# A hybrid attention trunk on one core: gate sums, logits and 1/rms from split fp32r parts, Silu and 1/rms by Ln and Exp

## The chip, the cores and the metric

The kernel runs on one core of one Trainium2 chip. The metric is the device time in microseconds (us) of one execution, and lower is better. TensorE (PE in the profile) multiplies matrices, VectorE (DVE) and ScalarE (ACT) work on tiles element by element, GpSimd (POOL) fills tiles and issues some loads, SyncE (SP) issues the loads of the large weights. TensorE's products land in PSUM, eight banks of 128 partitions by 512 fp32 columns; the other tiles live in SBUF.

## The reference

The input x has 512 tokens of 1024 features. Two layers run; every layer is FFN, mixer, FFN, each on a normed input and each added to x. The mixer is a gated linear attention (GLA) in layer 0 and a stick-breaking attention (SB) in layer 1. The last step is one more norm.

```python
def rmsnorm(x, g):
    y = x * lax.rsqrt(jnp.mean(x * x, axis=-1, keepdims=True) + EPS)
    return y * g

def swiglu(h, w_gate, w_up, w_down):
    return (jax.nn.silu(h @ w_gate) * (h @ w_up)) @ w_down

def gla_mixer(h, w_in, w_gk2, b_gk, o_norm, w_out):
    q, k, v, g, gk_lr = jnp.split(h @ w_in, [512, 1024, 2048, 3072], axis=-1)   # gk_lr: 16 columns
    log_a = jax.nn.log_sigmoid(gk_lr @ w_gk2 + b_gk) / 16.0
    ...                                     # four heads: o from q, k, v and the decay exp(cumsum(log_a))
    o = rmsnorm(o, o_norm)                  # over the 256 features of each head
    return (o * jax.nn.silu(g)) @ w_out
```

## The kernel before

**Layout.** x is held transposed: eight tiles `xs[k]` of 128 features by 512 tokens. A weight column block is the stationary operand of a product, the tokens are its moving operand, so a product has 512 columns. A norm needs a sum over features, which lie on partitions; that sum is made on TensorE with a tile of ones.

**Split operands.** A matrix product of fp32 values is made from three products of fp32r parts (`mm3`, line 66): an operand a is cast to fp32r (`high`), and `low` = a - high is the rest; high x high, low x high and high x low are added up in PSUM. ScalarE casts a weight block (line 124, `wh<-raw`) and VectorE subtracts (line 126, `wl<-raw,wh`). Some small products stay in plain fp32, among them the sums over features, the gate logits and the products inside the heads.

**The queue of weight blocks.** `Feed` holds a list of entries in order: each loads its block, splits it and multiplies. `feed.step` makes one part of the entry at the front, `feed.entries` makes whole entries, `two_halves` makes the first two of a stage in two halves each, so that the part that needs the later features comes last. Loads and splits run three to six entries ahead. Stages that have a chain of their own (the heads of the GLA, the SB) take steps of the feed in between, to keep TensorE supplied. The order in which the instructions of an engine are laid down comes from a scheduler at build time, by priority and by its own view of durations; on the chip each engine then works through its queue in that order.

**PSUM.** `psum(name, tag)` takes a page under the tags "a" (2 banks), "z" (3), "t" (2) and "o" (1); without a tag it goes round all eight in turn (line 47).

**The norm of a stage.** While the last product of a stage updates x, `prep` (line 368) multiplies x by the gain of the next norm, splits it, and `sumsq` (line 359) adds up the squares in `ss`. The next stage multiplies the un-normed input first and scales its first results by R, the 1/rms of each token spread over all partitions. `stats_a` (line 381) makes R's values: four products of `ss` with a ones column (ps_st, 512 tokens as 4 columns of 128 partitions), then `rstd` on tiles of 4 columns (Sqrt on ScalarE, reciprocal and one Newton step on VectorE). `stats_b` (line 421) spreads them: four 128x128 diagonal tiles `dg` times ones (ps_R), and a copy to `R`. This is done in each of six stages; the first FFN takes the sums from elsewhere.

**An FFN stage** (`FFN.run`, line 696) calls `two_halves(stats_a)`, `stats_b`, then scales the two products that waited, and in `normed_input` (line 644) makes the normed, split tiles that entries from the seventh on use (`nh`, `nl`).

**The GLA stage** (`GLA.run`, line 980). `gate_weights` loads the small gate weights by POOL. `gate_low` multiplies the 16 gate columns (ps_gk); they lie in rows 0 to 15 (high part of the weight) and 32 to 47 (low part). `gate_logits` multiplies by R into `ga` and makes the logits with the plain fp32 tile `w2` (ps_z, four products of 512 columns); row 64 is 1 for the bias. `evac_q`, `evac_k`, `evac_g` scale the products of a feature block (ps_f, tag "a") by R. q of heads 0 and 1 are the two that wait for R (`defer`), so they hold both banks "a". For each head, `levels` computes the scores in seven steps, `output` the head's result: squares, their sum by ones (ps_on, plain fp32, 512 columns), 1/rms by Ln, Exp and a Newton step, and the normed result `on`. `silu` (line 965) applies Silu to all eight gate tiles `gn` in head 3's turn, and `close` (line 971) multiplies `on` by `gn` and splits the product for `back`, the out projection (ps_b).

ScalarE holds one set of function tables at a time; a function from another set needs an `ACT_TABLE_LOAD`. `act` (line 459) keeps Exp and Ln behind the load of the set that has both.

Of the kernel before, what the change touches and what calls it, by code (L numbers as in the profile page):

```python
# [10 lines left out]
F32 = mybir.dt.float32  # L11
# [21 lines left out]
def decoder(ctx: ExitStack, tc: tile.TileContext, a: dict, out: bass.AP):  # L33
# [23 lines left out]
    gT = cp.tile([P, 51], F32, name="gT")  # L57
    nc.vector.memset(gT[:, 50:51], 1.0)
    ones = gT[:, 50:51].to_broadcast([P, P])

    xs = [xp.tile([P, T], F32, name=f"x{k}") for k in range(KD)]

# [71 lines left out]
    class Feed:  # L134
# [17 lines left out]
            e = self.q[i]  # L152
            return e.body(e.W)

        def step(self, n=1):
            while n > 0:
                if self.cur is None:
                    self.cur = self.start()
# [262 lines left out]
    def stats_b(tag=None):  # L421
# [12 lines left out]
        st["R"] = sp.tile([P, T], F32, tag="sq", name="R")  # L434
        nc.vector.tensor_copy(st["R"], ps)

    def two_halves(between=None):

        feed.finish()
        g = [feed.start(), feed.start()]  # L440
        for i in range(3):
            for x in g:
                next(x, None)
            if i == 0 and between is not None:
                between()
# [19 lines left out]
    class FFN:  # L465
# [9 lines left out]

        def __init__(self, wg, wu, wd, gi, nxt, first=False, last=False):
            self.gi, self.normed = gi, False
            self.defer, self.gates = [], []
            self.lead = []
            self.hs = [[] for _ in self.GROUPS]  # L480
            base, downs = len(feed.q), []
            self.sums_by = 10**6
            for group, (c0, c1) in enumerate(self.GROUPS):
                slots, put = 2 * (c1 - c0), 0
                if group == 1:

                    for put in range(self.AHEAD):
                        down(*downs[put], late=put == 0)
                    put = self.AHEAD
                for i in range(slots):  # L490
# [24 lines left out]
                    while c >= self.SEVEN and put < len(downs) * (i + 1) // slots:  # L515
                        down(*downs[put])
                        put += 1
                for x in downs[put:]:
                    down(*x)
                n = 2 * (c1 - c0)  # L520
                end = group + 1 == len(self.GROUPS)
                downs = [(wd, c0 * 256, n, self.hs[group], part, nxt if end else None) for part in range(n)]
            self.count = len(feed.q) - base
            if last:
                back_tok(wd, c0 * 256, n, self.hs[group], nxt)
            else:
                for x in downs:
                    down(*x)
            self.total = len(feed.q) - base
# [166 lines left out]
        def run(self, between=None):  # L696
            with tc.tile_pool(name="hp", bufs=8, reuse_waits="tile") as self.hp, tc.tile_pool(
# [1 line left out]
            ) as self.tp:  # L699
                st["few"] = self.hp  # L700
                new_norm()
                two_halves(stats_a)
                stats_b()
                flush(self.defer)
                def spread(todo, n):
                    for i in range(n):
# [21 lines left out]
    class GLA:  # L728
        def __init__(self, w_in, w_gk2, b_gk, og, w_out, nxt):
# [7 lines left out]
                feat(chunks[h // 2], h % 2, lambda ps: self.evac_q(h, ps), "a", self.defer if h < 2 else None)  # L737

            def kk(h):
                feat(chunks[2 + h // 2], h % 2, lambda ps: self.evac_k(h, ps), "a")  # L740

            qk(0), qk(1), kk(0), kk(1), qk(2), qk(3), kk(2), kk(3)
            for c in range(4):
# [25 lines left out]
        def evac_g(self, j, ps):  # L769
            self.gn[j] = self.gp.tile([P, T], F32, tag="g", name="gn")  # L770
            nc.vector.tensor_tensor(out=self.gn[j], in0=ps, in1=st["R"], op=ALU.mult)

        def gate_weights(self):

            gr = self.ep.tile([P, KD, 16], F32, tag="gr", bufs=1, name="gr")
            with nc.allow_non_contiguous_dma("gate columns"):
                nc.gpsimd.dma_start(gr, cols(self.w_in, 3072, 16))
            self.gs = gs = self.ep.tile([P, KD, P], F32R, tag="gs", bufs=1, name="gs")
            nc.gpsimd.memset(gs.bitcast(F32), 0.0)
            nc.scalar.copy(gs[:, :, 0:16], gr)  # L780
            nc.vector.tensor_tensor(
                out=gs[:, :, 32:48], in0=gr, in1=gs[:, :, 0:16].bitcast(F32), op=ALU.subtract
            )
            self.w2 = w2 = self.gp.tile([P, T], F32, tag="g", name="w2")
            nc.gpsimd.memset(w2, 0.0)
            nc.gpsimd.dma_start(w2[0:16], self.w_gk2)
            nc.gpsimd.dma_start(w2[32:48], self.w_gk2)
            nc.gpsimd.dma_start(w2[64:65], self.b_gk)
            self.tri = self.ep.tile([P, P], F32, tag="tri", bufs=1, name="tri")
            nc.gpsimd.dma_start(self.tri, a["c_tri"])  # L790
            lf = self.ep.tile([P, len(LEVELS) * P // 2], F32, tag="e", name="lf")
            nc.gpsimd.dma_start(lf, a["c_lvl"])
            self.lvl = self.ep.tile([P, len(LEVELS) * P // 2], U8, tag="lvl", bufs=1, name="lvl")
            nc.vector.tensor_copy(self.lvl, lf)
            self.ga = self.gp.tile([P, T], F32, tag="g", name="ga")
            nc.gpsimd.memset(self.ga[64:65], 1.0)

        def gate_low(self):
            self.psg = psum("ps_gk", "z")
# [2 lines left out]
                mm(self.psg, self.gs[:, k], st["l"][k], False, k == KD - 1)  # L802

        def gate_logits(self):
            nc.vector.tensor_tensor(
                out=self.ga[0:64], in0=self.psg[0:64], in1=st["R"][0:64], op=ALU.mult
            )
            self.la = []
            for i in range(NT):
                ps = psum("ps_z", "z")  # L810
                mm(ps, self.ga[0:65, i * P : (i + 1) * P], self.w2[0:65], True, True)
                t = self.gp.tile([P, T], F32, tag="g", name="la")
                nc.scalar.activation(t, ps, AF.Abs)
                act(t, t, AF.Exp, scale=-1.0)
# [70 lines left out]
        def output(self, h):  # L885
# [40 lines left out]
            for vb in range(2):  # L926
# [18 lines left out]
            nc.vector.tensor_scalar(  # L945
                out=vv, in0=ps, scalar1=1.0 / 256, scalar2=EPS, op0=ALU.mult, op1=ALU.add
# [15 lines left out]
                self.on[j] = t  # L962
            yield

        def silu(self):
            for j in range(KD):
                with tc.issue_after(st["last"]):
                    s = nc.scalar.activation(self.gn[j], self.gn[j], AF.Silu).ins
            exp_ln_tables(s)

        def close(self, h):
            for j in (2 * h, 2 * h + 1):
                nc.vector.tensor_tensor(out=self.on[j], in0=self.on[j], in1=self.gn[j], op=ALU.mult)
# [2 lines left out]
                nc.scalar.copy(hh, self.on[j])  # L976
                nc.vector.tensor_tensor(out=hl, in0=self.on[j], in1=hh.bitcast(F32), op=ALU.subtract)
                self.hs.append((hh, hl))

        def run(self):  # L980
            with ExitStack() as es:
# [17 lines left out]
                self.decay(0)  # L999
                self.decay(1)  # L1000
                prev = None
                for h in range(4):
                    if h == 1:
                        self.decay(2)
                        self.decay(3)
                    for n, _ in enumerate(self.levels(h)):
                        feed.step(1)
                        if prev is not None and n >= 1:
                            next(prev, None)
                            if n == 4:  # L1010
                                feed.step(1)
                    if prev is not None:
                        for _ in prev:
                            feed.step(1)
                    prev = self.output(h)
                    if h == 3:
                        while feed.pos < self.end:
                            feed.step(1)
                        feed.finish()
                        next(prev)  # L1020
                        self.silu()
                        for g in range(3):
                            self.close(g)
                for n, _ in enumerate(prev):
                    if n < 6:
                        feed.step(1)
                self.close(3)
                feed.entries(self.end + 2 - feed.pos)


# [338 lines left out]
```

## Time and profile before

| | us |
|---|---|
| median of 3 runs (1864.43 to 1865.8) | 1865.71 |
| the profiled execution | 1867.25 |
| its span, from the first to the last instruction | 1865.3 |
| PE busy | 1845.7 |
| DVE busy | 1409.8 |
| ACT busy | 1009.2 |

| stage | us from the span's start |
|---|---|
| first FFN | 0 to 351 |
| GLA | 351 to 595 |
| FFN, FFN | 595 to 933, 933 to 1271 |
| SB | 1271 to 1517 |
| last FFN and output | 1517 to 1865 |

A row of the timeline has the start, the duration, the engine, the line, the operation, output and inputs by name, the shapes, and how many were merged; a bracket says how long the engine had been idle before and what ended it. A product in plain fp32 leaves two records, one in fp32r leaves one; PEld is the load of the stationary operand, which overlaps the products. A group row ends with busy time and mean ns of one, then the idle time before the group and what ended it. Products are pipelined: each lasts longer in its record than its distance to the next, so the price of one in a stream is that distance.

### The profile page before, as it was taken

To read this page: it belongs to the slowest core of one execution; us is meant where nothing else is said; L and a number is where in the kernel's file an instruction comes from. 1 tells how busy PE (TensorE), PEld (TensorE's weight loads), DVE (VectorE), ACT (ScalarE), POOL (GpSimd) and SP (SyncE) were. 2 spreads that over 40 slices of the span, in tenths; PEclk is the share of its full clock that TensorE was granted. 3 is DMA by queue.
4 is the path that set the end of the run, shared out by engine and by line. 5 is a ranking of instruction groups with operands and counts; after the bars stand their busy time and mean duration, and the time that the engine had idled before them with its cause. 6 is when DMAs were issued, how large, how long until landed. Compare 5 with 4: busy or idle time off the path is not lost.

```text
span 1865.3 us, 29157 instructions
## 1 busy us (share of the span) xinstructions
PE 1845.7 (99%) x11945; PEld 1650.8 (88%) x11945; DVE 1409.8 (76%) x2171; ACT 1009.2 (54%) x1708; POOL 7.3 (0%) x17
## 2 busy tenths in 40 slices
PE   8999999999999999999999999999999999999998
PEld 6999999789888899999889999998888788999997
DVE  7987776675767987777788777676878669877775
ACT  6545445444555554544564445445888745554454
POOL 0000000000000000000000000000000000000000
PEclk9999999999999999999999999999999999999999
DMA  5343333211223233332243333233221222333321
GB/s 159 113 131 107 102 113 111 80 52 62 66 70 112 78 105 116 110 115 80 84 131 102 103 108 108 80 93 100 68 69 57 69 90 91 125 102 102 118 87 68
DMA packets 177513, 179.04 MB, mean 96 GB/s; under 512 B 4034, under 2 KB 167924, under 8 KB 177380
## 3 DMA queue, kind: packets, MB, share of 16 engines
q1 hardware_dynamic: 176768, 176.18, 29.7%
q8 instruction: 93, 1.52, 0.3%
q0 software_dynamic: 512, 0.99, 0.2%
q14 instruction: 40, 0.33, 0.1%
q10 hardware_dynamic: 100, 0.03, 0.0%
HBM read 175.11 MB, written 2.10 MB: 95 GB/s over the span
## 4 chain that ended last, share of the span: by engine, by line
PE 95%; DVE 2%; DMA 1%; ACT 1%; issue 0%; ACTq 0%; DVEq 0%; SPq 0%
PE ps_d L64 25%; PE ps_w L558 21%; PE ps_f L64 18%; PE ps_q L558 10%; PE ps_z L558 5%; PE ps_t L64 5%; PE ps_b L64 4%; PE ps_S L64 1%; PE ps_z L1093 1%; PE ps_bt L64 1%; PE ps_oT L1155 1%; PE ps_T L1140 1%; PE ps_o L64 1%; DMA raw<-in_ffn_w_up_dram 1%; DVE wl L126 0%; PE ps_R L431 0%
## 5 line engine op out<-in xcount | busy, mean ns | idle before, releaser
L126 DVE TENSOR_TENSOR wl<-raw,wh 128x1024 fp32r<-128x1024 f32 (+1 forms) x244 | 259.2, 1064 | 92.2 <-ACT wh L124 63.1
L124 ACT CAST wh<-raw 128x1024 fp32r<-128x1024 f32 (+1 forms) x244 | 224.8, 923 | 142.2 <-PE ps_f L64 44.3
L64 PE MATMUL ps_d<-hh,wl 128*128 128x512 f32 x672 | 262.1, 390 | 0.0
L64 PE MATMUL ps_d<-hh,wh 128*128 128x512 f32 x672 | 262.1, 390 | 0.0
L64 PE MATMUL ps_d<-hl,wh 128*128 128x512 f32 x672 | 261.4, 389 | 0.0
L558 PE MATMUL ps_w<-th,wh 128*128 128x256 f32 x864 | 238.9, 276 | 1.0 <-ACT u L600 1.0
L558 PE MATMUL ps_w<-tl,wh 128*128 128x256 f32 x864 | 238.6, 276 | 0.0
L558 PE MATMUL ps_w<-th,wl 128*128 128x256 f32 x864 | 238.6, 276 | 0.0
L124 ACT CAST wh<-s 128x1024 fp32r<-128x1024 f32 x144 | 151.1, 1049 | 121.9 <-PE ps_q L558 36.8
L126 DVE TENSOR_TENSOR wl<-s,wh 128x1024 fp32r<-128x1024 f32 x144 | 175.8, 1222 | 52.4 <-ACT wh L124 26.4
L318 DVE SCALAR_TENSOR_TENSOR x<-ps_d,x 128x512 f32<-128x512 f32 x184 | 124.7, 687 | 102.4 <-PE ps_d L64 101.8
L124 ACT CAST wh<-rawd 128x1024 fp32r<-128x1024 f32 x84 | 88.5, 1054 | 180.5 <-PE ps_d L64 98.1
L64 PE MATMUL ps_f<-xh,wh 128*128 128x512 f32 x448 | 181.5, 405 | 2.1 <-DVE q L756 1.5
L64 PE MATMUL ps_f<-xl,wh 128*128 128x512 f32 x448 | 175.1, 391 | 0.0
L64 PE MATMUL ps_f<-xh,wl 128*128 128x512 f32 x448 | 174.4, 389 | 0.0
L558 PEld LDWEIGHTS ps_w<-th,wh 128*128 128x128 f32 x864 | 162.2, 188 | 1.5 <-ACT u L600 1.4
L558 PEld LDWEIGHTS ps_w<-tl,wh 128*128 128x128 f32 x864 | 162.2, 188 | 0.0
L558 PEld LDWEIGHTS ps_w<-th,wl 128*128 128x128 f32 x864 | 162.2, 188 | 0.0
L64 PEld LDWEIGHTS ps_d<-hl,wh 128*128 128x128 f32 x672 | 126.2, 188 | 26.7
L64 PEld LDWEIGHTS ps_d<-hh,wh 128*128 128x128 f32 x672 | 126.1, 188 | 24.8
L64 PEld LDWEIGHTS ps_d<-hh,wl 128*128 128x128 f32 x672 | 126.1, 188 | 24.1
L126 DVE TENSOR_TENSOR wl<-rawd,wh 128x1024 fp32r<-128x1024 f32 x84 | 102.8, 1224 | 51.6 <-ACT wh L124 38.1
(253 smaller groups left out, 4431.8 us busy)
## 6 DMA issues: line engine op xcount, KB each, us to landing
raw<-in_ffn_w_gate_dram SPq DMA_DIRECT2D x43, 1024.0 KB, 5.4
raw<-in_ffn_w_up_dram SPq DMA_DIRECT2D x43, 1024.0 KB, 5.4
rawd<-in_ffn_w_down_dram SPq DMA_DIRECT2D x84, 512.0 KB, 3.5
raw<-in_gla_w_in_dram SPq DMA_DIRECT2D x12, 1024.0 KB, 5.5
raw<-in_sb_w_in_dram SPq DMA_DIRECT2D x16, 512.0 KB, 3.8
raw<-in_gla_w_out_dram SPq DMA_DIRECT2D x4, 1024.0 KB, 5.0
raw<-in_sb_w_in_dram SPq DMA_DIRECT2D x4, 1024.0 KB, 5.1
raw<-in_sb_w_out_dram SPq DMA_DIRECT2D x4, 1024.0 KB, 5.0
```

What stands on the lines that cost most here:

```text
L64: st["pe"] = nc.tensor.matmul(ps, l, r, start=first, stop=last).ins
L124: st["cut"] = nc.scalar.copy(h, r).ins
L126: nc.vector.tensor_tensor(out=l, in0=r, in1=h.bitcast(F32), op=ALU.subtract)
L318: nc.vector.scalar_tensor_tensor(out=xs[k], in0=ps, scalar=0.5, in1=xs[k], op0=ALU.mult, op1=ALU.add)
L558: st["pe"] = nc.tensor.matmul(o, l_, r_, start=first and j + n == 0, stop=j == 3 and n == 2, skip_group_check=True).ins
L1093: nc.tensor.matmul(o_, l_, r_, start=first, stop=last, skip_group_check=True)
L1140: nc.tensor.transpose(ps[:, c0 : c0 + P], ys[yb][:, yc + j * P : yc + (j + 1) * P], ident)
L1155: nc.tensor.matmul(po[e * 64 : e * 64 + 64, j * P : T], self.v[j][:, c : c + 64], self.wt[p, e][bk][:, c0 : c0 + n], start=j == 0, stop=j ...
```

## The change

It has five parts.

1. *R of three FFN stages* (the ones that follow the GLA, an FFN and the SB). `sums_wide` splits `ss` into high and low fp32r parts and multiplies each by ones, 128x128 out of one column, so that the sum stands on all partitions at once (ps_R, two products of 512 columns). `rstd_wide` makes 1/rms on 512 columns: v on VectorE, Ln, Exp and a Square on ScalarE, two VectorE steps for the Newton step. Between two FFNs the table set with Ln and Exp is loaded after the last Silu. `stats_a` and `stats_b` remain for the other three stages.
2. *Gate logits.* `ga` and `w2` become fp32r tiles with high and low parts in different rows, so that one product holds all parts.
3. *Sums of the heads' squares.* ps_on becomes two fp32r products of the high and low part with ones.
4. *Silu of the gate.* It is made in `evac_g` for each block from Abs, Exp, Ln and Exp on ScalarE and two more VectorE steps, with no other table set. `close` of a head runs as soon as its gate blocks and its output are there.
5. *A bank.* The first k block of the GLA takes its page from "o" and not from "a".

```diff
+    one_r = cp.tile([P, 16], F32R, name="one_r")[:, 0:1]
+    nc.scalar.copy(one_r, gT[:, 50:51])
+    ones_r = one_r.to_broadcast([P, P])
...
+    def sums_wide(pool):
+        ss = st["ss"]
+        h = sp.tile([P, T], F32R, tag="sq", name="sh")
+        nc.scalar.copy(h, ss)
+        l = pool.tile([P, T], F32R, tag="t", name="sl")
+        nc.vector.tensor_tensor(out=l, in0=ss, in1=h.bitcast(F32), op=ALU.subtract)
+        st["wide"] = ps = psum("ps_R")
+        mm(ps, ones_r, h, True, False)
+        mm(ps, ones_r, l, False, True)
+
+    def rstd_wide():
+        ps = st["wide"]
+        v = sp.tile([P, T], F32, tag="ss", name="v")
+        nc.vector.tensor_scalar(out=v, in0=ps, scalar1=1.0 / D, scalar2=EPS, op0=ALU.mult, op1=ALU.add)
+        y = st["R"] = sp.tile([P, T], F32, tag="sq", name="R")
+        act(y, v, AF.Ln)
+        act(y, y, AF.Exp, scale=-0.5)
+        nc.scalar.activation(ps, y, AF.Square)
+        nc.vector.scalar_tensor_tensor(out=v, in0=ps, scalar=-0.5, in1=v, op0=ALU.mult, op1=ALU.mult)
+        nc.vector.scalar_tensor_tensor(out=y, in0=v, scalar=1.5, in1=y, op0=ALU.add, op1=ALU.mult)
...
-                two_halves(stats_a)
-                stats_b()
+                if st["ss"] is None:
+                    two_halves(stats_a)
+                    stats_b()
+                else:
+                    if self.after_ffn:
+                        exp_ln_tables(st["silu"])
+                    two_halves(lambda: sums_wide(self.tp))
+                    rstd_wide()
...
-                feat(chunks[2 + h // 2], h % 2, lambda ps: self.evac_k(h, ps), "a")
+                feat(chunks[2 + h // 2], h % 2, lambda ps: self.evac_k(h, ps), "o" if h == 0 else "a")
...
             nc.vector.tensor_tensor(out=self.gn[j], in0=ps, in1=st["R"], op=ALU.mult)
+            s = self.ep.tile([P, T], F32, tag="s", bufs=2, name="sg")
+            nc.scalar.activation(s, self.gn[j], AF.Abs)
+            act(s, s, AF.Exp, scale=-1.0)
+            act(s, s, AF.Ln, bias=1.0)
+            nc.vector.scalar_tensor_tensor(
+                out=s, in0=self.gn[j], scalar=0.0, in1=s, op0=ALU.min, op1=ALU.subtract
+            )
+            act(s, s, AF.Exp)
+            nc.vector.tensor_tensor(out=self.gn[j], in0=self.gn[j], in1=s, op=ALU.mult)
+            self.gates = j + 1
...
-            nc.gpsimd.dma_start(w2[0:16], self.w_gk2)
-            nc.gpsimd.dma_start(w2[32:48], self.w_gk2)
-            nc.gpsimd.dma_start(w2[64:65], self.b_gk)
+            for r in range(0, P, 32):
+                nc.gpsimd.dma_start(w2[r : r + 16], self.w_gk2)
+            for r in (48, 112):
+                nc.gpsimd.dma_start(w2[r : r + 1], self.b_gk)
+            self.w2 = self.gp.tile([P, T], F32R, tag="g", name="w2r")
+            nc.scalar.copy(self.w2, w2)
+            low = slice(96, P)
+            nc.vector.tensor_tensor(out=self.w2[low], in0=w2[low], in1=self.w2[low].bitcast(F32), op=ALU.subtract)
...
-            nc.vector.tensor_tensor(
-                out=self.ga[0:64], in0=self.psg[0:64], in1=st["R"][0:64], op=ALU.mult
-            )
+            ga, t = self.ga, self.ep.tile([P, T], F32, tag="e", name="gl")
+            nc.vector.tensor_tensor(out=t[0:48], in0=self.psg[0:48], in1=st["R"][0:48], op=ALU.mult)
+            nc.scalar.copy(ga[0:48], t[0:48])
+            nc.vector.tensor_tensor(out=ga[64:80], in0=t[0:16], in1=ga[0:16].bitcast(F32), op=ALU.subtract)
+            nc.scalar.copy(ga[96:112], t[0:16])
...
-                mm(ps, self.ga[0:65, i * P : (i + 1) * P], self.w2[0:65], True, True)
+                mm(ps, ga[:, i * P : (i + 1) * P], self.w2, True, True)
...
+            sh = ep.tile([P, T], F32R, tag="e", name="sh")
+            sl = ep.tile([P, T], F32R, tag="e", name="sl")
+            nc.scalar.copy(sh, sq)
+            nc.vector.tensor_tensor(out=sl, in0=sq, in1=sh.bitcast(F32), op=ALU.subtract)
             ps = psum("ps_on", "o")
-            mm(ps, ones, sq, True, True)
+            mm(ps, self.ones, sh, True, False)
+            mm(ps, self.ones, sl, False, True)
...
-        def silu(self):
-            for j in range(KD):
-                with tc.issue_after(st["last"]):
-                    s = nc.scalar.activation(self.gn[j], self.gn[j], AF.Silu).ins
-            exp_ln_tables(s)
...
+        def close_ready(self):
+            while self.closed < min(self.outs, self.gates // 2):
+                self.close(self.closed)
+                self.closed += 1
```

`run` of the GLA calls `close_ready` after every step of the feed, and no longer calls `silu` and the three closings together in head 3's turn.

More of the change, by code (lines that the diff above doesn't have):

```diff
@@ L153, in start, with step @@
             return e.body(e.W)
-        def step(self, n=1):
+        def step(self, n=1, end=None):
             while n > 0:
                 if self.cur is None:
+                    if self.pos == end:
+                        return
                     self.cur = self.start()
@@ L477, in __init__ @@
             self.gi, self.normed = gi, False
+            self.after_ffn = bool(phases) and isinstance(phases[-1], FFN)
             self.defer, self.gates = [], []
@@ L783, in gate_weights @@
             )
-            self.w2 = w2 = self.gp.tile([P, T], F32, tag="g", name="w2")
+            w2 = self.gp.tile([P, T], F32, tag="g", name="w2")
             nc.gpsimd.memset(w2, 0.0)
-            nc.gpsimd.dma_start(w2[0:16], self.w_gk2)
-            nc.gpsimd.dma_start(w2[32:48], self.w_gk2)
-            nc.gpsimd.dma_start(w2[64:65], self.b_gk)
+            for r in range(0, P, 32):
[6 more added lines that the diff above has]
+            nc.vector.tensor_tensor(out=self.w2[low], in0=w2[low], in1=self.w2[low].bitcast(F32), op=ALU.subtract)
+            one = self.ep.tile([P, 64], F32R, tag="one", bufs=1, name="one")[:, 0:1]
+            nc.scalar.copy(one, gT[:, 50:51])
+            self.ones = one.to_broadcast([P, P])
             self.tri = self.ep.tile([P, P], F32, tag="tri", bufs=1, name="tri")
@@ L794, in gate_weights @@
             nc.vector.tensor_copy(self.lvl, lf)
-            self.ga = self.gp.tile([P, T], F32, tag="g", name="ga")
-            nc.gpsimd.memset(self.ga[64:65], 1.0)
+            self.ga = self.gp.tile([P, T], F32R, tag="g", name="ga")
+            nc.gpsimd.memset(self.ga.bitcast(F32), 1.0)
         def gate_low(self):
@@ L978, in close, with step @@
                 self.hs.append((hh, hl))
+        def step(self, n=1):
+            feed.step(n, self.end)
+            self.close_ready()
+        def close_ready(self):
+            while self.closed < min(self.outs, self.gates // 2):
+                self.close(self.closed)
+                self.closed += 1
         def run(self):
@@ L1001, in run @@
                 prev = None
+                self.closed = self.outs = self.gates = 0
                 for h in range(4):
@@ L1006, in run @@
                     for n, _ in enumerate(self.levels(h)):
-                        feed.step(1)
+                        self.step()
                         if prev is not None and n >= 1:
@@ L1010, in run @@
                             if n == 4:
-                                feed.step(1)
+                                self.step()
                     if prev is not None:
                         for _ in prev:
-                            feed.step(1)
+                            self.step()
+                        self.outs = h
                     prev = self.output(h)
                     if h == 3:
+                        next(prev)
                         while feed.pos < self.end:
-                            feed.step(1)
+                            self.step()
                         feed.finish()
[L1020 to L1023, printed above, removed]
+                        self.close_ready()
                 for n, _ in enumerate(prev):
@@ L1026, in run @@
                         feed.step(1)
-                self.close(3)
+                self.outs = 4
+                self.close_ready()
                 feed.entries(self.end + 2 - feed.pos)
```

## The prediction

> **What bounds the kernel now.** I read the page first: span, busy time, the chain that ended last.
>
> ```profile
> span 1865.3 us, 29157 instructions
> PE 1845.7 (99%) x11945; PEld 1650.8 (88%) x11945; DVE 1409.8 (76%) x2171; ACT 1009.2 (54%) x1708; POOL 7.3 (0%) x17
> PE 95%; DVE 2%; DMA 1%; ACT 1%; issue 0%; ACTq 0%; DVEq 0%; SPq 0%
> ```
>
> TensorE is busy almost throughout and carries 95% of the chain. Next, the list of what TensorE waited for, because a busy share alone hides small holes:
>
> ```profile
> PE ps_g L1290 <- DMA gl<-in_ffn_norm_dram: 5.6, 1, 5.6
> PE ps_f L64 <- DVE q L756: 1.5, 1, 1.5
> PE ps_x L1297 <- DMA x<-in_x_dram: 1.0, 4, 0.4
> PE ps_o L64 <- DVE on L959: 0.6, 1, 0.6
> PE ps_b L64 <- ACT oh L976: 0.6, 1, 0.6
> PE ps_st L64 <- DVE ss L366: 0.3, 1, 0.3
> ```
>
> Columns: total, times, longest (us). After the first load little is lost: the kernel is a queue of products. So a product taken out of the queue is worth its own time, as long as the work added on VectorE and ScalarE is done before TensorE asks for it.
>
> **Products taken out.** The price of a fp32r product of 512 columns comes from the chain's long run of ps_f; those of the old statistics from the timeline:
>
> ```profile
> 608.39 32.68 PE ps_f L64 x144
> ```
> ```profile
> 362.55 0.95 PE L64 MATMUL ps_st<-gT,ss 128*128 128x1 f32 x8
> 363.36 0.48 PE L64 MATMUL ps_gk<-xh,gs 128*128 128x512 f32 x1
> ...
> 602.93 1.05 PE L64 MATMUL ps_st<-gT,ss 128*128 128x1 f32 x8 [0.34 <-DVE ss L366]
> ...
> 607.34 1.05 PE L431 MATMUL ps_R<-dg,gT 128*128 128x128 f32 x8
> 608.15 0.48 PE L64 MATMUL ps_f<-xh,wh 128*128 128x512 f32 x1
> ```
>
> One fp32r product: 32.68/144 = 0.227. The statistics of one stage: ps_st 363.36-362.55 = 0.81, ps_R 608.15-607.34 = 0.81. In their place stand two fp32r products, 0.453. Three stages: 3 x (1.62-0.45) = 3.5 us.
>
> The gate logits ps_z and the norm sums ps_on are fp32 products that become fp32r:
>
> ```profile
> 371.66 0.19 PEld L64 LDWEIGHTS ps_z<-w,ga 65*128 65x128 f32 x1 [0.24 <-issue]
> 372.09 0.19 PEld L64 LDWEIGHTS ps_z<-w,ga 65*128 65x128 f32 x1 [0.24 <-issue]
> 372.52 0.19 PEld L64 LDWEIGHTS ps_z<-w,ga 65*128 65x128 f32 x1 [0.24 <-PE ps_z L64]
> ...
> 566.49 1.02 PE L64 MATMUL ps_on<-osq,gT 128*128 128x512 f32 x2
> 567.57 0.39 PE L64 MATMUL ps_b<-oh,wl 128*128 128x512 f32 x1
> ```
>
> Each fp32 product has two passes 0.43 apart, 0.857 together; ps_on agrees (567.57-566.49 less one fp32r product = 0.85). Four ps_z to one fp32r product each: 4 x (0.857-0.227) = 2.5. Four ps_on to two each: 4 x (0.857-0.453) = 1.6. Products together: 7.6 us.
>
> A page bears on the new products' price. The Trainium skill (TensorE: Matmul & The Clock Gate, Back-to-back issue gap) gives about 131 ns per product of 512 columns in a sustained stream. By that figure the 18 new products would take 1.7 us less and the gain would be 9.3; the 144 products above took 227 ns each, and the row decides.
>
> **The wait at the start of the linear attention.** Both "a" banks hold q until R is there, and the first k product waits for one:
>
> ```profile
> 368.26 0.69 DVE L435 COPY R<-ps_R 128x512 f32<-128x512 f32 x1 [1.03 <-PE ps_R L431]
> 368.98 1.29 DVE L756 SCALAR_TENSOR_TENSOR q<-ps_f,R 128x512 f32<-128x512 f32 x2
> 369.73 0.50 PE L64 MATMUL ps_f<-xh,wh 128*128 128x512 f32 x1 [1.51 <-DVE q L756]
> 370.19 0.67 DVE L805 TENSOR_TENSOR ga<-ps_gk,R 64x512 f32<-64x512 f32 x1
> ```
>
> With the first k in bank "o" the 1.5 us go. What is late next is ga: after its multiplication by R come a cast, a subtraction and a cast, three links of about 0.65. R comes 0.23 later (one product now stands ahead of ps_R): 369.2, q to 370.4, the product to 371.1, ga complete at about 372.4. In the built order 19 products lie between ps_R and the first ps_z, which TensorE reaches at 367.4+0.81+19 x 0.227 = 372.5. So the work just fits; the fourth ps_z waits for its bank until the first la is done, some 0.3. I charge 0.3, at most 1.5 (the old wait back). The three extra loads and the cast of w2 lie on POOL, ACT and DVE ahead of the opening and are done before R.
>
> **Openings of the three FFN stages.** The path from the last sum to R, in the opening at 602 and then the one at 1523:
>
> ```profile
> 602.18 0.69 DVE L366 TENSOR_TENSOR ss<-ss,sq 128x512 f32<-128x512 f32 x1 [0.70 <-ACT sq L365]
> 608.43 0.69 DVE L435 COPY R<-ps_R 128x512 f32<-128x512 f32 x1 [0.95 <-PE ps_R L431]
> ...
> 1523.50 0.95 PE L64 MATMUL ps_st<-gT,ss 128*128 128x1 f32 x8
> 1530.25 0.69 DVE L435 COPY R<-ps_R 128x512 f32<-128x512 f32 x1 [1.30 <-PE ps_R L431]
> ...
> L462 ACT ACTIVATE y<-vv 128x512 f32<-128x512 f32 x4 | 2.5, 632 | 5.6 <-DVE vv L945 5.4
> ...
> 1551.80 1.30 DVE L641 TENSOR_TENSOR nl<-xn,nh 128x512 fp32r<-128x512 f32 x2
> 1551.85 0.39 PE L64 MATMUL ps_f<-nh,wh 128*128 128x512 f32 x1
> ```
>
> At 602.93 TensorE waited for the sum (0.34 in its row). Now it waits for the cast sh behind that sum, one link more (0.62), with three products put in between (0.68): the wait stays as it was. From the sum's end, 602.87: sh to 603.5, sl to 604.2, the second product read out at 604.7, v to 605.4, a weight cast of 1.05 that stands ahead of Ln to 605.9, then Ln, Exp, Square, two VectorE steps of 0.69: R at 609.1, as before (608.43+0.69).
>
> At 1523 the products stand ten behind the old sums: 1525.8, the second done at 1526.9; v to 1527.6; Ln, a weight cast (1.05), Exp, Square to 1530.5; two VectorE steps to 1531.9. R came at 1530.94, and TensorE is 1.17 earlier: 2.1 less cover. The old cover: the low part of block 3 is done at 1552.5 and asked for three groups (0.68 each) and two products after 1551.85, at 1554.35: 1.85. A stall of 0.3 here. At 602 only the 1.17 of cover is lost, and at the third opening, between two FFNs, no weight cast stands ahead of Ln and R comes about a microsecond earlier by the same count: no stall at either. Without the cover each would cost up to 2.1.
>
> **Costed at nothing.** The Ln and Exp table is loaded between two FFNs right after the last Silu, in the long run of ps_d; one load (1.28) would show if ScalarE were late there, which the wait list doesn't have. With one PSUM page fewer per stage the page order shifts: at the last opening the first two ps_f take banks "t" and "o", which the out projection's accumulators left last. The second ps_f starts twelve products, 2.7 us, after the first, and two x updates of about 0.7 free its bank in 1.4; without that cover 1.4. SP's queue holds the same loads in the same order, and a load starts when its weight cast is done, so it follows the engines.
>
> **The added work of the gate.** Silu becomes four ACT steps and two more DVE steps per block, between the products of the last two heads:
>
> ```profile
> core 0: us, PE busy (x) PEld busy (x) DVE busy (x) ACT busy (x) POOL busy (x), PEclk, DMA share, GB/s
> 486.00:548.00 62.00, 60.76 (x336) 50.49 (x334) 43.51 (x81) 42.97 (x55) 0.00 (x0) 1.00 0.16 52
> 608.00:640.00 32.00, 32.00 (x145) 26.51 (x143) 31.15 (x54) 20.90 (x32) 0.00 (x0) 1.00 0.26 81
> ...
> 547.37 2.49 DVE L977 TENSOR_TENSOR ol<-on,oh 128x512 fp32r<-128x512 f32 x4
> ...
> L968 ACT ACTIVATE gn<-gn 128x512 f32<-128x512 f32 x8 | 5.1, 631 | 0.9 <-DVE gn L771 0.8
> L968 ACT ACT_TABLE_LOAD x5 | 6.4, 1283 | 0.1
> L462 ACT ACT_TABLE_LOAD x7 | 9.0, 1283 | 0.9 <-DVE e L847 0.8
> ...
> 544.10 0.50 PE L64 MATMUL ps_b<-oh,wh 128*128 128x512 f32 x1 [0.56 <-ACT oh L976]
> 546.86 1.21 PE L64 MATMUL ps_o<-S,v 128*128 128x128 f32 x6 [0.64 <-DVE on L959]
> ```
>
> ScalarE breaks even: 24 more steps of about 0.6 are 14, against 12 table loads of 1.28 that fall away here, 15. VectorE queues 512-column steps 0.60 apart ((2.49-0.69)/3): 16 gate steps 9.6, two sl 1.2, some six closing steps that move ahead of the burst at 547, 3.6. That makes 43.5+14.4 = 57.9 of some 61 us (less two ps_on savings): 95% full. Full VectorE stretches are covered when the order suits, as the row 608:640 shows (31.15 of 32, no TensorE wait). Bounds: gain of 1.2 if the two waits of the last rows go because the closings come earlier; loss of 18.5 (62-43.5) if all the old VectorE idle stays on top of the new work, less the room of 3.1, so 15.4. I take 1.0, near the covered end, since the order was laid for these lengths.
>
> The new cast at the start puts a table load ahead of the gl loads, 0.8 us later; the transposes behind them wait for x anyway (the 1.0 above). Zero; 0.8 without that cover.
>
> **Sum.** -7.6 -1.5 +0.3 +0.3 +1.0 = -7.5 us. The profiled execution took 1867.25 us (span 1865.3 and 1.95 around it), 1.5 above the median 1865.71 of the runs shown; from the median: 1858.2.
>
> **Rivals.**
> - *All of it and the closing waits too:* -7.6-1.5-1.2 = -10.3, 1855.4. For it: TensorE is so dense that nothing else is left to wait for. Against: VectorE at 95%.
> - *VectorE half bound:* half of its old idle, 9.2, stays: 9.2-3.1 = 6.1 late, in all -3.0: 1862.7. For it: its idle in the stretch was mostly waiting for TensorE and ScalarE, and the gate chain crosses between engines four times. Against: eight blocks interleave.
> - *VectorE's queue becomes the bound (slower):* each gate step that stands ahead of its Exp or Ln holds all scores of the head behind it, so all 18.5 stay: 15.4-9.1 = +6.3, 1872.0. It decides from 12.2 us of idle kept (3.1+9.1). For it: one queue in program order, a 95% stretch. Against: the same queue at 97% in 608:640. The Trainium skill (TensorE: Matmul & The Clock Gate, the table at its head) calls VectorE's queue strict first-in first-out; by that rule nothing behind a waiting step can pass it.
> - *R too late at the openings:* 2.1 at each of three, 6.3 against the 0.3 charged: -1.5, 1864.2. For it: 97% VectorE behind R. Against: 1.85 of cover counted.
>
> **How the numbers follow.** A measurement of this kernel tells about 0.2% (3.7 us) from no change, so faster is below 1862.0. Forecast 0.62, all of it 0.18: faster 0.80. Half bound 0.09 and openings 0.05: within 0.14. Queue as bound 0.06: slower. The range, 1854 to 1863.5, holds the first three cases' places; the top leaves out the late openings and the slower case.
>
> **What would show it.** Right: ps_on in eight records near 390 ns where it had eight near 600, ps_z in four; ps_st only 16; no wait of ps_f for q; 12 table loads instead of 27. Wrong: new TensorE waits over 1 us for DVE e, S or gn between the first gate block and the end of the out projection; ps_f of an FFN opening waiting for DVE nl; ps_R waiting for sl.

## The result and the profile after

| | before | after |
|---|---|---|
| median, us | 1865.76 (1864.43 to 1866.89, 6 runs) | 1854.74 (1853.66 to 1855.58, 6 runs) |
| profiled execution | 1867.25 | 1854.57 |

The ratio is 0.9941 with an interval of 0.9928 to 0.9954: 11.0 us less, well clear of no change. The forecast was 1858.2, 7.5 us less; the rival "all of it and the closing waits too" stood at 1855.4.

The page of the changed kernel, the lines on span, busy time and chain:

```profile
span 1852.6 us, 29092 instructions
PE 1836.5 (99%) x11899; PEld 1645.3 (89%) x11899; DVE 1421.5 (77%) x2172; ACT 1012.7 (55%) x1735; POOL 8.8 (0%) x20
PE 95%; DVE 2%; ACT 2%; DMA 1%; issue 0%; SPq 0%; ACTq 0%; DVEq 0%
```

TensorE still carries the chain. It is busy 9.2 us less in a span that is 12.7 us shorter, so products went, and waits with them. (1.5 of the 12.7 belong to the profiled execution of before, which lay that much above its median. Most of that may be one wait in an FFN behind a weight load that took 6.6 us; it stands in the list of waits of before but not among the rows that the prediction shows of it.) That row, and then all of what TensorE waited for after:

```profile
PE ps_w L558 <- ACT u L600: 1.0, 1, 1.0
```
```profile
PE ps_g L1360 <- DMA gl<-in_gla_o_norm_dram: 6.5, 1, 6.5
PE ps_x L1367 <- DMA x<-in_x_dram: 0.9, 2, 0.7
PE ps_oT L1225 <- ACT wt L490: 0.6, 2, 0.4
PE ps_w L587 <- ACT ps_z L611: 0.4, 2, 0.2
PE ps_z L1163 <- DVE r L1196: 0.2, 1, 0.2
```

No row is left for q, for the closings (oh, on) or for an FFN opening. The groups of instructions by shape show the products that were swapped (count, then busy us and mean ns):

```profile
L67 PE MATMUL ps_st<-gT,ss 128*128 128x1 f32 x16 | 1.9, 239 | 0.0
L67 PE MATMUL ps_on<-sh,one 128*128 128x512 f32 x4 | 1.8, 446 | 0.1
L67 PE MATMUL ps_on<-sl,one 128*128 128x512 f32 x4 | 1.7, 423 | 0.0
L67 PE MATMUL ps_z<-w2r,ga 128*128 128x512 f32 x4 | 1.4, 432 | 0.0
L67 PE MATMUL ps_R<-sh,one_r 128*128 128x512 f32 x3 | 1.4, 462 | 0.1
L67 PE MATMUL ps_R<-sl,one_r 128*128 128x512 f32 x3 | 1.4, 450 | 0.0
```

The timeline of the changed kernel at the start and the end of the GLA stage, and then the two rows of before that answer to the last two (its first ps_gk, 363.36, stands in the prediction):

```profile
363.05 0.48 PE L67 MATMUL ps_gk<-xh,gs 128*128 128x512 f32 x1
...
370.12 0.67 DVE L864 TENSOR_TENSOR gl<-ps_gk,R 48x512 f32<-48x512 f32 x1
371.53 0.68 DVE L866 TENSOR_TENSOR ga<-gl,ga 16x512 fp32r<-16x512 f32 x1 [0.74 <-ACT ga L865]
...
372.36 0.93 PE L67 MATMUL ps_z<-w2r,ga 128*128 128x512 f32 x3
...
376.32 0.47 PE L67 MATMUL ps_z<-w2r,ga 128*128 128x512 f32 x1
...
379.83 1.50 PE L67 MATMUL ps_d<-tri,la 128*128 128x128 f32 x12
...
587.31 0.39 PE L67 MATMUL ps_f<-xh,wh 128*128 128x512 f32 x1
```
```profile
384.47 1.95 PE L64 MATMUL ps_d<-tri,la 128*128 128x128 f32 x16
...
594.95 0.39 PE L64 MATMUL ps_f<-xh,wh 128*128 128x512 f32 x1
```

Such rows cut the span into parts, each from the first product of a stage to that of the next. The last column but one is a second trace of the changed kernel (the run "changed again" below), which shows how well a part repeats.

| part, us | before | after | again | forecast change |
|---|---|---|---|---|
| first ps_f to first ps_gk | 348.70 | 348.20 | 348.45 | 0 |
| ps_gk to the first ps_d of the GLA | 21.11 | 16.78 | 16.77 | -2.5 -1.5 +0.3 = -3.7 |
| from there to the next FFN | 210.48 | 207.48 | 207.16 | -1.6 +1.0 = -0.6 |
| FFN | 337.68 | 336.35 | 337.07 | -1.2 |
| FFN (before: with the late load) | 338.48 | 335.62 | 335.60 | -1.2 |
| SB | 246.27 | 246.17 | 246.92 | 0 |
| last FFN, output | 347.94 | 347.19 | 347.39 | -1.2 +0.3 = -0.9 |

The third line is where the forecast was short: -3.0 to -3.3 against -0.6. The stretch of the last two heads, cut at the same place in the work (before 486 to 547; after, five us earlier; columns as in the prediction), before and then after:

```profile
486.00:547.00 61.00, 59.80 (x330) 49.80 (x329) 42.51 (x79) 41.97 (x53) 0.00 (x0) 1.00 0.16 53
```
```profile
481.00:542.00 61.00, 61.00 (x340) 51.59 (x340) 54.23 (x99) 38.81 (x64) 0.00 (x0) 1.00 0.16 54
```

VectorE took 11.7 us more, not 14.4, and TensorE has no idle time at all; ScalarE took 3.2 less.

### The profile page after: what moved, and what is told of

Its sections match the earlier page's. It is cut to its first block, busy times and chain, and to the rows that moved or that the text cites. A ratio compares the mean times of both kernels' runs of the same rounds, so it can differ in the third digit from the quotient of the medians.

```text
span 1852.6 us, 29092 instructions
## 1 busy us (share of the span) xinstructions
PE 1836.5 (99%) x11899; PEld 1645.3 (89%) x11899; DVE 1421.5 (77%) x2172; ACT 1012.7 (55%) x1735; POOL 8.8 (0%) x20
## 4 chain that ended last, share of the span: by engine, by line
PE 95%; DVE 2%; ACT 2%; DMA 1%; issue 0%; SPq 0%; ACTq 0%; DVEq 0%
PE ps_d L67 25%; PE ps_w L587 21%; PE ps_f L67 18%; PE ps_q L587 10%; PE ps_z L587 5%; PE ps_t L67 5%; PE ps_b L67 4%; PE ps_S L67 1%; PE ps_bt L67 1%; PE ps_z L1163 1%; PE ps_oT L1225 1%; PE ps_T L1210 1%; PE ps_o L67 1%; DMA x<-in_x_dram 1%; ACT wh L127 0%; DVE wl L129 0%
```

## The experiments

A median carries some 2.3 us either way (the intervals), more than most terms. So each run is also read by the two GLA lines of the table, which repeat within 0.5 in kernels that should agree there.

| run | median, us | ratio to before | ps_gk to ps_d | ps_d to FFN |
|---|---|---|---|---|
| changed again | 1855.72 | 0.9941 [0.9929, 0.9954] | 16.77 | 207.16 |
| old statistics | 1858.22 | 0.9957 [0.9944, 0.9969] | 16.75 | 207.19 |
| fp32 logits | 1857.74 | 0.9954 [0.9942, 0.9967] | 19.35 | 207.02 |
| fp32 norm sums | 1857.43 | 0.9952 [0.9940, 0.9965] | 16.74 | 208.72 |
| bank "a" | 1857.49 | 0.9949 [0.9936, 0.9961] | 18.47 | 207.54 |
| before, bank "o" alone | 1865.17 | 0.9990 [0.9981, 0.9999] | 19.36 | 210.40 |
| before, gate's part alone | 1863.93 | 0.9985 [0.9976, 0.9994] | 21.13 | 208.47 |
| VectorE +9.6 us | 1860.16 | 0.9962 [0.9949, 0.9976] | 16.78 | 211.34 |
| VectorE +19.2 us | 1875.83 | 1.0049 [1.0037, 1.0062] | 16.76 | 228.59 |
| Silu table, late closings | 1862.89 | 0.9984 [0.9975, 0.9993] | 16.76 | 214.40 |
| Exp Silu, late closings | 1857.22 | 0.9949 [0.9937, 0.9962] | 16.77 | 208.72 |
| Silu table, early closings | 1863.13 | 0.9979 [0.9970, 0.9988] | 16.82 | 213.78 |

**Parts one, two, three undone, one at a time**, in the changed kernel.

> The changed kernel with the old statistics (ps_st, rstd on 4 columns, dg, ps_R) in the three FFN stages; all else as changed. Theory A (TensorE is a queue of products, every opening stays covered): the three stages get back 3 x 1.17 = 3.5 us, so about 1858.2 against 1854.7. Theory B (the longer path to R costs part of the gain at the openings): less than 2 us come back, below 1856.7.

```diff
-                if st["ss"] is None:
+                if True:
                     two_halves(stats_a)
```

> The changed kernel with ga and w2 in plain fp32 as before, four fp32 products ps_z. Theory A: 4 x 0.63 = 2.5 us come back, about 1857.2. Theory B (the three links more that ga now needs hold TensorE): 1 us or less comes back, about 1855.7.

```diff
-            self.w2 = self.gp.tile([P, T], F32R, tag="g", name="w2r")
...
-            self.ga = self.gp.tile([P, T], F32R, tag="g", name="ga")
+            self.ga = self.gp.tile([P, T], F32, tag="g", name="ga")
...
-                mm(ps, ga[:, i * P : (i + 1) * P], self.w2, True, True)
+                mm(ps, self.ga[0:65, i * P : (i + 1) * P], self.w2[0:65], True, True)
```

> The changed kernel with ps_on as one plain fp32 product per head. Theory A: 4 x 0.40 = 1.6 us come back, about 1856.3. Theory B (the extra cast and subtraction on the head's path cost as much as the products save): no difference, 1854.7.

```diff
-            nc.scalar.copy(sh, sq)
-            nc.vector.tensor_tensor(out=sl, in0=sq, in1=sh.bitcast(F32), op=ALU.subtract)
...
-            mm(ps, self.ones, sh, True, False)
-            mm(ps, self.ones, sl, False, True)
+            mm(ps, ones, sq, True, True)
```

Logits: the first line grew by 2.58, the second not: 2.5 was forecast. Norm sums: the second grew by 1.2 to 1.6 (1.6). Old statistics: the GLA is unchanged. Whole FFN stages repeat too badly for a term of 1.2 (the last one took from 347.2 to 347.9 in kernels that should agree there), so the three openings are read from the first product of the stage to the first one on a normed tile (nh). In the last stage these are the first two rows for the changed kernel, and the other two with the old statistics:

```profile
1505.45 0.39 PE L67 MATMUL ps_f<-xh,wh 128*128 128x512 f32 x1
1538.84 0.39 PE L67 MATMUL ps_f<-nh,wh 128*128 128x512 f32 x1
```
```profile
1506.21 0.39 PE L67 MATMUL ps_f<-xh,wh 128*128 128x512 f32 x1
1540.69 0.39 PE L67 MATMUL ps_f<-nh,wh 128*128 128x512 f32 x1
```

That is 33.39 against 34.48. The other two openings took 34.75 and 34.52 with the old statistics; the changed kernel's two traces have 33.53 and 33.72 for the one, 33.33 and 33.30 for the other. So the openings gave 1.0 to 1.2, 1.2 and 1.1, in all 3.4 to 3.5 of the forecast 3.5. Theory A holds in all three runs; by the medians alone, with their 2.3 either way, it could not be told from Theory B.

**The bank**, taken back in the changed kernel, and alone in the kernel before.

> The changed kernel with the first k block's page from bank a again. Theory A: TensorE waits 1.5 us for DVE q again, about 1856.2. Theory B (the path of ga is what holds TensorE there now, so that the bank doesn't matter): within 0.3 of 1854.7.

> The kernel before, with part five alone: the first k block of the linear attention takes its page from bank o. Theory A (the parts add up): the wait of ps_f for DVE q (1.5 us) is gone and the time is 1.5 us less than before. Theory B (in the kernel before, the chain to the out projection's first operand sits just behind TensorE, so what TensorE gains ahead of it turns into a longer wait there): the wait of 1.5 is gone, the waits of ps_b for ACT oh and ps_o for DVE on grow from 1.2 together to 2 us or more, and the time is within 0.7 us of before.

```diff
-                feat(chunks[2 + h // 2], h % 2, lambda ps: self.evac_k(h, ps), "a")
+                feat(chunks[2 + h // 2], h % 2, lambda ps: self.evac_k(h, ps), "o" if h == 0 else "a")
```

The lists of waits, first with bank "a" put back, then of the kernel before with bank "o" alone:

```profile
PE ps_f L67 <- DVE q L792: 1.5, 1, 1.5
```
```profile
PE ps_o L64 <- DVE on L959: 0.7, 1, 0.7
PE ps_b L64 <- ACT oh L976: 0.6, 1, 0.6
```

Put back, the wait returns and the first line grows by 1.69; alone, the line shrinks by 1.75 and the closings wait as long as they did. Theory A holds in both runs. The gain is whole without the other parts: Theory B, which had it vanish into a longer wait at the out projection, fell. Both numbers are above the row's 1.51. The products' records overlap (0.39 long, 0.227 apart), and a wait is counted from the end of the record before, so a wait in a stream costs 0.16 more than its row: 1.67.

**The gate's part alone**, put into the kernel before: Silu by Abs, Exp, Ln, Exp and the early closings, with all products and banks as before.

> The kernel before with the gate's part alone: Silu by Abs, Exp, Ln and Exp per block, closings as soon as they can run. Theory A as the forecast had it: 1.0 us slower than before. Theory B (it removes the closing waits): 1.2 us faster than before, and no wait for ACT oh and DVE on.

```diff
-                        self.silu()
-                        for g in range(3):
-                            self.close(g)
+                        self.close_ready()
```

The second line shrank by 2.0 and the waits for oh and on are gone from the list, with this in the stretch of the last two heads:

```profile
486.00:547.00 61.00, 60.99 (x337) 51.26 (x336) 53.50 (x98) 37.94 (x63) 0.00 (x0) 1.00 0.16 54
```

VectorE has 53.5 of 61, and TensorE idles for nothing (60.99, against 59.80 before). Theory A, a small loss, was wrong in sign; Theory B holds, with 2.0 where it had 1.2. The two closing waits give 0.56+0.64 and twice 0.16, 1.5 of the 2.0; the last 0.5 has no row. The part takes the table loads away and makes the closings early, both at once; which of the two ended the waits in the kernel before, no run separates. With the norm sums' 1.2 to 1.6 this makes 3.2 to 3.6, and 3.0 to 3.3 was the whole change of that line: the parts add up from the side of before.

**How much room VectorE has.** Two, then four more VectorE steps of 512 columns per gate block, whose results nobody uses, in the changed kernel.

> The changed kernel with two more VectorE steps of 512 columns per gate block, written to a tile that nothing reads: 16 x 0.60 = 9.6 us more on VectorE between the first and the last gate block. Theory A (VectorE at 89% of that stretch in the changed kernel, 55.2 of 62, so 6.8 free, and what does not fit is paid): 2.8 us slower, about 1857.5. Theory B (VectorE's idle time cannot be used, all is paid): 9.6 slower, 1864.3. Theory C (the order spreads the work past the stretch): no difference.

> The same with four more VectorE steps per gate block, 32 x 0.60 = 19.2 us. Theory A: 19.2-6.8 = 12.4 us slower, about 1867. Theory B: 1874. Theory C: no difference.

```diff
             nc.vector.tensor_tensor(out=self.gn[j], in0=self.gn[j], in1=s, op=ALU.mult)
+            for _ in range(2):
+                junk = self.ep.tile([P, T], F32, tag="jk", bufs=1, name="jk")
+                nc.vector.tensor_tensor(out=junk, in0=self.gn[j], in1=self.gn[j], op=ALU.mult)
```

9.6 us more on VectorE cost 4.0 (second line; 3.9 to 4.2), so a little over half was covered: Theory A, with 2.8, is the nearest. The largest wait that came is 1.3, of ps_o for on. 19.2 cost 21.3, more than was added and more than any theory had. The largest waits with four steps, and two stretches of its windows:

```profile
PE ps_b L67 <- DVE gn L807: 4.8, 1, 4.8
PE ps_S L67 <- DVE e L913: 4.2, 3, 2.9
PE ps_kd L971 <- DVE kd L961: 2.8, 1, 2.8
```
```profile
525.87:532.69 6.82, 6.74 (x22) 5.92 (x23) 6.82 (x15) 2.93 (x5) 0.00 (x0) 0.50 0.36 118
549.76:563.41 13.65, 7.94 (x22) 5.89 (x23) 13.65 (x21) 4.77 (x8) 0.00 (x0) 0.50 0.08 19
```

Now the large waits are all for VectorE, among them those that the rival "VectorE's queue becomes the bound" named: S's scores (e) and gn. With two small ones of the same stretch (0.6 for kt, 0.3 for wl) they make 12.7, and 0.16 for each of the seven 1.1. Then the clock: it was granted at 0.50 in these two stretches, in which TensorE worked 6.74 and 7.94 us, so half of that, 7.3 us, was lost to it. The sum is 21.1 of the 21.3. So the mechanism is real, and its full price, all that is added, sets in between 9.6 and 19.2 us of VectorE work beyond the change.

**What the gate's part is worth in the changed kernel.** Three kernels with all the other parts as changed: Silu from its own table set and the three closings together in head 3's turn, as before; the new Silu with those late closings; and Silu from its own table set at each block with the early closings.

> The changed kernel with Silu from its own table set and the closings of heads 0 to 2 together in head 3's turn, as before. Theory A as the forecast had it (the gate's steps on VectorE cost 1.0 us): the time falls to about 1853.7. Theory B (the gate's part removes the two waits at the closings): 1.2 us come back, about 1855.9, and TensorE waits again for ACT oh and DVE on.

> The changed kernel, with Silu made from Abs, Exp, Ln and Exp as there, but the closings of heads 0 to 2 all in a row in head 3's turn, as before the change. The run with Silu from its own table set and these late closings lost 7.7 us. Theory A (the table loads in ScalarE's queue, ahead of the casts that the out projection waits for, are what cost it): without them the late closings cost little, at most 1 us against the changed kernel, and TensorE's wait for ACT oh at the out projection stays under 0.6 us. Theory B (it is the burst of three closings at the end that VectorE and ScalarE cannot finish in time): 5 to 8 us slower than the changed kernel, with a wait of 3 us or more ahead of the first ps_b.

> The changed kernel, with Silu of each gate block from Silu's own table set as soon as the block is there, and closings as early as in the changed kernel. Two table loads of 1.28 us for each block or pair of blocks come into ScalarE's queue between the heads' Exp and Ln; VectorE has 16 steps fewer, 9.6 us. Theory A (table loads cost): 8 to 16 loads, 10 to 20 us of ScalarE's time in the stretch of the last two heads, and TensorE waits there for ACT or for what hangs on it: 4 us or more slower than the changed kernel. Theory B (the burst costs): within 1 us of the changed kernel, for the closings are early and VectorE has less to do.

```diff
             nc.vector.tensor_tensor(out=self.gn[j], in0=ps, in1=st["R"], op=ALU.mult)
-            s = self.ep.tile([P, T], F32, tag="s", bufs=2, name="sg")
...
-            nc.vector.tensor_tensor(out=self.gn[j], in0=self.gn[j], in1=s, op=ALU.mult)
+            with tc.issue_after(st["last"]):
+                nc.scalar.activation(self.gn[j], self.gn[j], AF.Silu)
```

(The diff is that of the third. The closings are moved by the edit shown for the gate's part alone, in reverse.) Both theories missed on the first: it cost 6.9 to 7.2 in the GLA, far over the 2.0 that the part gave alone. The second cost 1.2 to 1.6, the third 6.3 to 6.6. So most of it is the table loads, and a smaller part comes with the late closings. In the later two runs Theory A is the right one, though its bound for the second was 1: TensorE has no wait for oh there, and its one wait in the heads is 1.15, for kt, with the overlap 1.3. How late closings make kt late isn't shown. The first kernel's ScalarE queue ahead of the out projection, in the timeline, and the cast of the kernel before that answers to its cast of oh:

```profile
534.41 1.28 ACT L490 ACT_TABLE_LOAD   x1
...
536.35 1.28 ACT L490 ACT_TABLE_LOAD   x1
...
538.71 1.28 ACT L1022 ACT_TABLE_LOAD   x1
...
541.68 1.28 ACT L485 ACT_TABLE_LOAD   x1
542.97 2.18 ACT L1030 CAST oh<-on 128x512 fp32r<-128x512 f32 x4
...
543.64 0.50 PE L67 MATMUL ps_b<-oh,wh 128*128 128x512 f32 x1 [4.28 <-ACT oh L1030]
```
```profile
543.44 1.13 ACT L976 CAST oh<-on 128x512 fp32r<-128x512 f32 x2
```

Four loads, 5.1 us of 8.6, stand ahead of the cast that TensorE waits 4.28 for. With 0.8 for e, 0.16 for each of the two and 1.7 for the clock (below), that is 7.1 of the 6.9 to 7.2. In the kernel before, the same queue had three loads ahead of that cast, and TensorE, whose last product ahead of the wait stood 4.2 us later (543.27 against 539.10), waited 0.56. The cast itself came at nearly the same time in both, 543.44 and 542.97: with the loads in the queue, most of what the other parts had gained ahead of it turned into the wait. So the gate's part was worth 2.0 alone and 7 beside the others. The third kernel is hit elsewhere: two groups of its table loads in the GLA, 18 in all where Theory A had counted 8 to 16, then VectorE's and TensorE's rows:

```profile
L490 ACT ACT_TABLE_LOAD x11 | 14.1, 1283 | 0.4 <-DVE vv L1002 0.3
L809 ACT ACT_TABLE_LOAD x7 | 9.0, 1283 | 0.1
```
```profile
500.13 0.69 DVE L1024 TENSOR_TENSOR on<-on,gn 128x512 f32<-128x512 f32 x1 [2.07 <-ACT gn L809]
...
505.46 0.42 DVE L902 TENSOR_TENSOR e<-e,q 128x256 f32<-128x256 f32 x1
506.03 0.65 PE L67 MATMUL ps_S<-e 128*64 128x64 f32 x8 [2.02 <-DVE e L902]
```

A closing step waited 2.07 for a gate block whose Silu stood behind a load, and the scores e stood behind it in VectorE's queue. The Trainium skill (TensorE: Matmul & The Clock Gate, the table at its head) calls that queue strict first-in first-out; these rows agree. The three TensorE waits of this kernel, for e (2.0), on (1.4) and kt (0.8), make 4.2; with 0.16 for each and 1.7 for the clock, 6.4 of the 6.3 to 6.6. What stays open: the order of the instructions is laid anew for every kernel, so 6 to 7 us is the price of the loads in these two orders and not in every one.

**The changed kernel again**, beside the last three.

> The changed kernel once more, beside the other three on one chip, so that each is compared with it as well as with the kernel before: ratio to the kernel before 0.993 to 0.995.

The ratio is the first one to the fourth digit.

## Why the prediction came out as it did

- *Products and bank, -7.6 and -1.5: right.* Undone one by one, the logits gave 2.58, the norm sums 1.2 to 1.6, the statistics 3.4 to 3.5 and the bank 1.7, in all 8.9 to 9.4 of 9.1. The forecast list came true: 16 ps_st, eight ps_on records of 391 to 501 ns, four ps_z, 12 table loads for 27, no wait for q.
- *The ga path, +0.3: 0.* ga was complete at 372.21 and TensorE there at 372.36, as the count had it (372.4 and 372.5). The fourth ps_z did not wait for its bank: the built order had put it fourteen ps_f later, at 376.32, which the charge overlooked.
- *The opening at 1523, +0.3: 0.* No ps_f waited for nl, and that opening gave 1.1 like the others. The rows of the changed kernel's timeline (its first ps_f there stands at 1505.45), and the stage's first ps_f in that of before:

```profile
1512.90 0.43 PE L67 MATMUL ps_R<-sl,one_r 128*128 128x512 f32 x1
...
1517.59 0.69 DVE L463 SCALAR_TENSOR_TENSOR R<-v,R 128x512 f32<-128x512 f32 x1
```
```profile
1517.38 0.39 PE L64 MATMUL ps_f<-xh,wh 128*128 128x512 f32 x1
```

  Counted from that ps_f, R was ready 13.6 us in before (1530.94), 12.8 after, and 14.5 in the count. The count put the second new product's end at 9.5 (1526.9); it came at 7.9, because the new products stood not ten products behind the old sums' place but two and five. That is 1.6 of the 1.7 between count and measurement.
- *The added work of the gate, +1.0: the mis-sized term.* The part gave 2.0 in the kernel before. The prediction set the covered end at -1.2 (both closing waits gone), called it a rival, and chose +1.0 because VectorE would be 95% full. So its sign was wrong: the waits that it left standing went. VectorE was 89% full (54.23 of 61), for the early closings hardly moved work into the stretch (54.23 or, again, 54.60 us with them, 53.40 without, where 3.6 had been charged). And a wait costs 0.16 more than its row. The 3.0 between +1.0 and -2.0, with the two charges of 0.3, is 3.6, about what the forecast was short by (3.5). The range, 1854 to 1863.5, held 1854.7 with 0.7 to spare, because it was drawn to take in that rival's place, 1855.4.
- *The rivals.* "All of it and the closing waits too" was the case. "Half bound" and "queue as bound" did not come; in the runs with more VectorE work the first price came within 9.6 us of further work, the full one between 9.6 and 19.2. "R too late" did not come: the three openings gave what their products cost.
- *ScalarE "breaks even":* it gained 3.2 in the stretch. In the two kernels with the loads put back, what counted was not the sum but where the loads stood, ahead of casts and scores. The prediction priced the loads as busy time alone.
- *Costed at nothing:* the start stayed as it was. The first ps_f came at 14.85, before at 14.66, though ps_g had waited 0.9 longer.

## What to carry to other kernels

Where TensorE is full, products taken out pay their distance in the stream, and a wait pays its row plus the overlap of the records. Work added to another engine is priced by who is queued behind it: here 18 table loads of 1.28 us in a queue that TensorE's inputs stand in cost 6.3 to 6.6 us, though VectorE had 9.6 us less to do. Before charging a full engine, count the steps that really land in the stretch, and test its room by adding work.

## What the runs showed of the hardware

TensorE's granted clock fell to one half after a wait of two us or more, which no term had. The windows of the kernel with Silu's table and late closings, around its wait of 4.28, and of the one with early closings, around its wait of 2.02:

```profile
542.00:543.00 1.00, 0.00 (x0) 0.00 (x0) 0.96 (x2) 0.99 (x2) 0.00 (x0) 1.00 0.00 0
...
544.00:545.00 1.00, 1.00 (x4) 0.81 (x3) 1.00 (x2) 1.00 (x3) 0.00 (x0) 0.57 0.00 0
...
547.00:548.00 1.00, 1.00 (x5) 0.81 (x4) 1.00 (x2) 0.45 (x1) 0.00 (x0) 0.72 0.00 0
```
```profile
506.50:507.00 0.50, 0.50 (x5) 0.36 (x4) 0.50 (x2) 0.00 (x0) 0.00 (x0) 0.97 0.00 0
507.00:508.00 1.00, 1.00 (x9) 1.00 (x7) 1.00 (x4) 0.80 (x2) 0.00 (x0) 0.50 0.00 0
...
510.00:510.50 0.50, 0.50 (x3) 0.47 (x2) 0.50 (x2) 0.09 (x1) 0.00 (x0) 0.62 0.00 0
```

In both the clock is full through the idle time, falls some 0.5 to 0.9 us after the products have started again, and stays at half for about 3.4 us: 544.1 to 547.6 (from the shares 0.57 and 0.72) and 507.0 to 510.4. That is 1.7 us of work lost each time. In the kernel with 19.2 us more on VectorE the two stretches at half (525.9 to 532.7 and 549.8 to 563.4) lasted 6.8 and 13.7 us, about two and four times 3.4. The first began as the products started again after the wait of 2.9 (525.95), so the delay of 0.5 to 0.9 is not a fixed one. After the wait of 1.5 in the kernel before, the clock stayed at 1.00. The Trainium skill (TensorE: Matmul & The Clock Gate, Part 1: The HAM clock gate) has the clock halve after at least one idle window of about 3.4 us and come back after a busy one; the 3.4 us agree, but here a wait of 2.0 was enough.
